# Strassen's algorithm for gate and up of a SwiGLU, and a down projection that adds in DRAM

## The chip, the core and the metric

The kernel runs on one core of one Trainium2 chip. The metric is device time in microseconds of one execution, the median of several runs. A core has five engines with instruction streams of their own: TensorE (PE in the profile; PEld is its weight load), VectorE (DVE), ScalarE (ACT), GpSimd (POOL) and SyncE (SP, which here only issues DMAs). Each takes its instructions in order, and semaphores tie them together.

## The reference

One decoder layer over 512 tokens in float32, width 2048. Two token mixers (windowed attention and gated linear attention) are merged and projected, and then comes the part that the change touches, a SwiGLU with 5632 hidden features:

```python
h = h + merged @ w_out[l]
z = rmsnorm(h, norm_ffn_g[l])
ff = (jax.nn.silu(z @ w_ffn_gate[l]) * (z @ w_ffn_up[l])) @ w_ffn_down[l]
h = h + ff
return rmsnorm(h, norm_final_g)
```

## The kernel before

Features lie on the 128 partitions and the 512 tokens on the free axis, so an activation is 16 tiles of 128x512. TensorE works on operands of about 12 significant bits (fp32r). Each float32 operand is therefore split into a high part (`wh`, `zh`, `fh`: a ScalarE cast) and a low part (`wl`, `zl`, `fl`: a VectorE subtraction), and each product takes three matmuls: hi x hi, hi x lo, lo x hi (`mm3`).

All weights come from DRAM as pieces of 128x1024 (512 KB), in the order of their use, on SP's queue. `load_piece` issues the DMA into `wf` and splits it into `wh` and `wl`; `next_piece` hands out a piece and asks for the second one behind it. There are three buffers of each kind. `project` makes two feature tiles out of four pieces: 24 matmuls of 512 tokens per piece.

The SwiGLU takes the hidden features in `NB` = 11 blocks of 512. `ffn_up` makes gate and up of a block in two halves of two feature tiles each (gate's two tiles, then up's two), with sigmoid and products behind them, and splits the result into `fh`, `fl`. `ffn_down` multiplies a block by the 512x2048 rows of the down weight, 16 output tiles of 12 matmuls, and VectorE adds each tile to `acc`, which stays in SBUF and is loaded from `h_d` (the residual, in DRAM) in block 0. The loop makes `ffn_up(blk + 1)` ahead of `ffn_down(blk)`, so that TensorE has work while a block's elementwise part ends. The last block goes by halves of 256 tokens. Its weights (`wfd`, `whd`, `wld`) are loaded and split while `ffn_down` of block 9 runs, and each half ends in the final norm.

The residual, the gained second-norm input `z` and its split are made behind the output projection `wo`, tile by tile (`hT`, `zh`, `zl`, and `hsq`, the sum of squares). The norm's inverse rms (`second_norm`) is applied behind the products. SBUF for activations is a pool of 66 long slots ("slot") and 12 short ones ("work") of 128x512. PSUM has four banks for products (`psm`) and four others. A scheduler orders the instructions of each engine, so the order in a queue isn't quite that of the code.

Of the kernel before, what the change touches and what calls it, by code (L numbers as in the profile page):

```python
# [19 lines left out]
P = 128  # L20
# [28 lines left out]
N_LONG, N_SHORT = 66, 12  # L49
# [4 lines left out]
def shape_constants():  # L54
    """Arrays that the shapes alone fix: which bias bucket a distance falls in, and masks."""
# [25 lines left out]
def weight_pieces(w_in, w_proj_a, w_proj_b, w_out, w_ffn_gate, w_ffn_up, w_ffn_down):  # L81
    """The weights in the order of their use, in pieces of [128, 1024]: partition p of a piece holds
    rows p, p + 128, ... of some rows and columns of a weight."""
# [30 lines left out]
    def up(blk):  # L114
        for c0 in (blk * T, blk * T + 2 * P):
            pair(w_ffn_gate, c0)
            pair(w_ffn_up, c0)

    up(0)
    for blk in range(NB):  # L120
        if blk + 1 < NB:
            up(blk + 1)
        for c0 in range(0, D, 2 * P):
            cut(w_ffn_down, blk * T, c0, 4, 2 * P)
    return np.stack(pieces)
# [3 lines left out]
def hybrid_layer(  # L129
# [24 lines left out]
    wpool = ctx.enter_context(tc.tile_pool(name="wpool", bufs=3))  # L154
# [6 lines left out]
    def slot(name, dtype=F32):  # L161
        return tpool.tile([P, T], dtype, tag="t", name=name)
# [23 lines left out]
    # the first use of ScalarE loads its table: ahead of the data  # L186
# [7 lines left out]
    def split(dst_hi, dst_lo, src):  # L194
        """src = hi + lo exactly, each of 12 significant bits."""
        nc.scalar.copy(dst_hi, src)  # L196
        nc.vector.tensor_tensor(out=dst_lo, in0=src, in1=dst_hi.bitcast(F32), op=ALU.subtract)  # L197

    n_last = D // (2 * P)
    n_pieces = pieces.shape[0] - n_last  # L200
    ahead = []

    def load_piece(i):
        wf = wpool.tile([P, CW], F32, tag="wf", name=f"wf_{i}")
        wh = wpool.tile([P, CW], F32R, tag="wh", name=f"wh_{i}")
        wl = wpool.tile([P, CW], F32R, tag="wl", name=f"wl_{i}")
        ahead.append((wh, wl))
        if i < KD // 2:
            return wf
        nc.sync.dma_start(wf, pieces[i])  # L210
        split(wh, wl, wf)

    taken = [0]
# [15 lines left out]
    def mm3(ps, ah, al, bh, bl, first, last):  # L229
        """ps += (ah + al).T @ (bh + bl)."""  # L230
# [4 lines left out]
    def project(rh, rl, name):  # L235
        """Two banks of (w[:, 256 columns].T @ r), features on partitions."""
# [11 lines left out]
    def inv_rms(ssq, n, name, cols=4):  # L248
        """(ssq / n + eps) ** -0.5 on a [128, cols] tile."""
# [8 lines left out]
    def across(r, name, cols=4):  # L258
        """[128 tokens, cols] -> a bank with the tokens' values on every partition."""
        bank = aux_bank(f"ps_b_{name}")  # L260
        for tt in range(cols):
            diag = small.tile([P, P], F32, tag="diag", name=f"diag_{name}_{tt}")
# [6 lines left out]
    def token_sums(sqs, name, cols=4):  # L269
        """Column sums of the sum of [128, 128 * cols] tiles, as [128 tokens, cols] in a bank."""  # L270
# [287 lines left out]
    def log_gates():  # L558
        """log(sigmoid(z)) = min(z, 0) - log(1 + exp(-|z|)), head by head."""
# [20 lines left out]
    def gla_values(c):  # L580
        """Values of heads 2c and 2c+1, tokens on partitions."""
# [15 lines left out]
    def scaled(banks, name):  # L597
        """What a projection left in banks, times each token's inverse rms."""
# [13 lines left out]
    def gla_gate(h, q, k, st):  # L612
        """Decayed queries and keys of a head, from its log gates summed in chunks."""
# [13 lines left out]
        # of each chunk in a pair: what its queries see a state through, what its keys reach one  # L627
        # through; and the pair's whole decay
# [30 lines left out]
    def gla_scores(h, st):  # L659
        """Scores inside a pair of chunks, keys on partitions; the state's keys, tokens there."""  # L660
# [25 lines left out]
    def gla_states(h, vs, st):  # L686
        """The state ahead of each pair of chunks."""
# [23 lines left out]
    def gla_outputs(h, vs, st):  # L711
        """Outputs, features on partitions, and their inverse rms."""
# [75 lines left out]
    def gated(yh, yl, m0, name):  # L788
        """sigmoid(gate) * (y @ w) for two feature tiles."""
# [29 lines left out]
    zh, zl = [], []  # L819
    hsq = slot("hsq")  # L820
    for m0 in range(0, KD, 2):
        for i, bank in enumerate(project(mh, ml, f"wo{m0}")):
# [5 lines left out]
            zh.append(slot(f"zh_{m}", F32R))  # L828
            zl.append(slot(f"zl_{m}", F32R))
            gcol = g_ffn_sb[:, m : m + 1]  # L830
            nc.scalar.activation(zh[m], hT, AF.Copy, scale=gcol)
            nc.vector.scalar_tensor_tensor(
                out=zl[m],
                in0=hT,
                scalar=gcol,
                in1=zh[m].bitcast(F32),
                op0=ALU.mult,
                op1=ALU.subtract,
            )
            if m == 0:  # L840
                nc.scalar.activation(hsq, hT, AF.Square)
            else:
                s2 = work(f"hsq_{m}")
                nc.scalar.activation(s2, hT, AF.Square)
                nc.vector.tensor_tensor(out=hsq, in0=hsq, in1=s2, op=ALU.add)

    def second_norm():
        rb = slot("rb2")
        nc.vector.tensor_copy(rb, across(inv_rms(token_sums([hsq], "ffn"), D, "ffn"), "ffn"))
        return rb  # L850

# [1 line left out]
    acc = [None] * KD  # L853
    rb2 = None

    def ffn_up(blk):
        fh, fl = [], []
        for pair in range(2):
            gs = []
            banks = project(zh, zl, f"fg{blk}_{pair}")  # L860
            if blk == 0 and pair == 0:
                nonlocal rb2
                rb2 = second_norm()
            for m, bank in enumerate(banks):
                g = work(f"g_{blk}_{pair}_{m}")
                nc.vector.tensor_tensor(out=g, in0=bank, in1=rb2, op=ALU.mult)
                s = work(f"gs_{blk}_{pair}_{m}")
                nc.scalar.activation(s, g, AF.Sigmoid)
                nc.vector.tensor_tensor(out=g, in0=g, in1=s, op=ALU.mult)
                gs.append(g)  # L870
            for m, bank in enumerate(project(zh, zl, f"fu{blk}_{pair}")):
                u = work(f"u_{blk}_{pair}_{m}")
                nc.vector.tensor_tensor(out=u, in0=bank, in1=rb2, op=ALU.mult)
# [142 lines left out]
```

## Time and profile before

| | |
|---|---|
| median of 3 runs | 2664.93 us (2664.81 to 2666.26) |
| the profiled execution | a span of 2663.9 us, the time of its engines' work; 2664.93 is 1.0 above it |
| TensorE | 99% of the span busy, clock 0.996 |
| VectorE, ScalarE, GpSimd | 45%, 28%, 1% |
| DMA | 280.73 MB, mean 105 GB/s |
| wf loads | 448 of 512 KB, median 3.7 us to landing |
| one SwiGLU block | 576 matmuls of 512 tokens, 0.2266 us from start to start (5296 in 1200 us): 130.5 us, a third of it the down projection |

The page gives totals first, then the span in 40 slices, the DMA queues, the chain of work that ended last, and the costliest groups. A row of a group ends in the count, the busy time, the mean duration in ns, and the idle time of the engine just ahead of it with what ended that. In a timeline row the start and the duration (us) come first. A row of a table by stretches gives each engine's busy time with its number of instructions in brackets, then the TensorE clock, the DMA share of 16 engines and GB/s. In a row on an operation's durations, three numbers are least, median and largest ns.

### The profile page before, as it was taken

The numbers are of one execution on the slowest core, as the hardware profiler recorded it, in microseconds if no ns is written. First come the engines' busy times: TensorE is split into PE (matmuls) and PEld (weight loads), VectorE is DVE, ScalarE is ACT, GpSimd is POOL, SyncE is SP. The second block draws the span as 40 slices with busy tenths as digits, with TensorE's granted clock in tenths as the row PEclk, the third lists the DMA queues.
The fourth block names the chain that finished last, engine by engine and source line by source line (L and its number), as shares of the span: only waits on it lengthen the run. The fifth ranks groups of instructions, "written<-read, shape, count | busy, mean of one in ns | idle before, by whom it ended". The sixth has DMA issues, their size and how long they took to land.

```text
span 2663.9 us, 29245 instructions
## 1 busy us (share of the span) xinstructions
PE 2635.0 (99%) x12038; PEld 2188.5 (82%) x12038; DVE 1185.7 (45%) x1690; ACT 753.0 (28%) x1040; POOL 21.4 (1%) x42
## 2 busy tenths in 40 slices
PE   8899999999999999999999999999999999999998
PEld 7777888888888888888888888888888888888887
DVE  6695463733333335444343434444434343434355
ACT  5465222422222223332222222222222222222233
POOL 0000000000000000000000000000000000000001
PEclk9999999999999999999999999999999999999999
DMA  6622223234433333443343233323323232233231
GB/s 193 130 71 71 80 87 95 72 127 133 127 111 111 108 98 107 142 147 103 99 141 117 95 98 101 95 95 96 102 95 95 96 101 96 95 96 102 95 124 67
DMA packets 92070, 280.73 MB, mean 105 GB/s; under 512 B 10512, under 2 KB 18880, under 8 KB 91936
## 3 DMA queue, kind: packets, MB, share of 16 engines
q1 hardware_dynamic: 91936, 278.87, 33.3%
q8 instruction: 94, 1.54, 0.2%
q14 instruction: 40, 0.33, 0.0%
HBM read 263.11 MB, written 15.72 MB: 105 GB/s over the span
## 4 chain that ended last, share of the span: by engine, by line
PE 96%; DMA 1%; DVE 1%; ACT 1%; issue 0%; POOL 0%; SPq 0%; DVEq 0%; ACTq 0%; POOLq 0%
PE ps_fd L232 6%; PE ps_fd L233 6%; PE ps_fd L231 6%; PE ps_fg L233 6%; PE ps_fg L231 6%; PE ps_fg L232 6%; PE ps_fu L233 6%; PE ps_fu L232 6%; PE ps_fu L231 6%; PE ps_ga L231 2%; PE ps_wo L233 2%; PE ps_gb L231 2%; PE ps_ga L232 2%; PE ps_wo L232 2%; PE ps_ga L233 2%; PE ps_gb L233 2%
## 5 line engine op out<-in xcount | busy, mean ns | idle before, releaser
L197 DVE TENSOR_TENSOR wl<-wf,wh 128x1024 fp32r<-128x1024 f32 (+1 forms) x464 | 559.0, 1205 | 1011.0 <-ACT wh L196 1002.6
L196 ACT CAST wh<-wf 128x1024 fp32r<-128x1024 f32 (+1 forms) x464 | 481.3, 1038 | 1535.6 <-PE ps_fd L232 315.5
L231 PE MATMUL ps_fu<-zh,wh 128*128 128x512 f32 x704 | 274.0, 389 | 0.0
L232 PE MATMUL ps_fu<-zl,wh 128*128 128x512 f32 x704 | 274.0, 389 | 0.0
L233 PE MATMUL ps_fu<-zh,wl 128*128 128x512 f32 x704 | 273.9, 389 | 0.0
L231 PE MATMUL ps_fg<-zh,wh 128*128 128x512 f32 x704 | 273.9, 389 | 0.0
L232 PE MATMUL ps_fg<-zl,wh 128*128 128x512 f32 x704 | 273.9, 389 | 0.0
L233 PE MATMUL ps_fg<-zh,wl 128*128 128x512 f32 x704 | 273.9, 389 | 0.0
L231 PE MATMUL ps_fd<-fh,wh 128*128 128x512 f32 x640 | 249.0, 389 | 0.0
L232 PE MATMUL ps_fd<-fl,wh 128*128 128x512 f32 x640 | 249.0, 389 | 0.0
L233 PE MATMUL ps_fd<-fh,wl 128*128 128x512 f32 x640 | 249.0, 389 | 0.0
L892 DVE TENSOR_TENSOR acc<-ps_fd,acc 128x512 f32<-128x512 f32 x160 | 110.5, 691 | 193.7 <-PE ps_fd L233 193.7
L232 PEld LDWEIGHTS ps_fg<-zl,wh 128*128 128x128 f32 x704 | 132.2, 188 | 27.4
L233 PEld LDWEIGHTS ps_fu<-zh,wl 128*128 128x128 f32 x704 | 132.2, 188 | 27.4
L233 PEld LDWEIGHTS ps_fg<-zh,wl 128*128 128x128 f32 x704 | 132.2, 188 | 27.4
L232 PEld LDWEIGHTS ps_fu<-zl,wh 128*128 128x128 f32 x704 | 132.2, 188 | 27.4
L231 PEld LDWEIGHTS ps_fg<-zh,wh 128*128 128x128 f32 x704 | 132.2, 188 | 27.4
L231 PEld LDWEIGHTS ps_fu<-zh,wh 128*128 128x128 f32 x704 | 132.2, 188 | 27.4
L231 PEld LDWEIGHTS ps_fd<-fh,wh 128*128 128x128 f32 x640 | 120.2, 188 | 25.0
L233 PEld LDWEIGHTS ps_fd<-fh,wl 128*128 128x128 f32 x640 | 120.2, 188 | 24.9
L232 PEld LDWEIGHTS ps_fd<-fl,wh 128*128 128x128 f32 x640 | 120.2, 188 | 24.9
L231 PE MATMUL ps_ga<-uh,wh 128*128 128x512 f32 x256 | 100.1, 391 | 0.0
(264 smaller groups left out, 3992.8 us busy)
## 6 DMA issues: line engine op xcount, KB each, us to landing
wf<-in_pieces_dram SPq DMA_DIRECT2D x448, 512.0 KB, 3.7
x<-in_xT_dram SPq DMA_DIRECT2D x16, 256.0 KB, 4.8
wf<-in_pieces_dram SPq DMA_DIRECT2D x16, 256.0 KB, 4.6
mA_d<-sga SPq DMA_DIRECT2D x16, 256.0 KB, 3.2
ya<-mA_d SPq DMA_DIRECT2D x16, 256.0 KB, 3.0
hT<-in_xT_dram SPq DMA_DIRECT2D x16, 256.0 KB, 3.6
h_d<-hT SPq DMA_DIRECT2D x16, 256.0 KB, 3.3
acc<-h_d SPq DMA_DIRECT2D x16, 256.0 KB, 4.8
```

The lines of the kernel that those rows point to most:

```text
L196: nc.scalar.copy(dst_hi, src)
L197: nc.vector.tensor_tensor(out=dst_lo, in0=src, in1=dst_hi.bitcast(F32), op=ALU.subtract)
L231: nc.tensor.matmul(ps, lhsT=ah, rhs=bh, start=first, stop=False)
L232: nc.tensor.matmul(ps, lhsT=ah, rhs=bl, start=False, stop=False)
L233: nc.tensor.matmul(ps, lhsT=al, rhs=bh, start=False, stop=last)
L892: nc.vector.tensor_tensor(out=acc[m], in0=bank, in1=acc[m], op=ALU.add)
```

## The change

Gate and up are computed by Strassen's algorithm for 2x2 blocks, in Winograd's form with seven products. The two halves of the tokens are the columns of one operand. The other operand is made of two feature tiles (even and odd) of the input by the two weights, gate and up. Each product has 256 tokens. A piece now holds a "quad": four 128-row tiles of gate and of up for one hidden tile.

- Weights. `load_quads` splits three of the four raw blocks (768 columns), makes four sums of 256 columns in place on VectorE, and splits all 1024 columns again into `th` and `tl`. `wh` and `wl` have four buffers, of which a quad takes two each; `wf` has two.
- Tokens. `strassen_side` makes from each pair of feature tiles of `z` four sums and seven split sides (`zs`) of 256 tokens. Three pairs (`KEPT` = 6 tiles) go into the output projection, five behind it. The norm of the mixers (`rb1`) is applied to `z`, and `second_norm` divides it out again.
- Products. `ffn_pair(blk, j)` makes one hidden tile of gate and up out of four quads: 7 x 2 x 3 = 42 matmuls of 256 tokens per quad, 168 per pair. It needs all four banks of `psm`. A ScalarE copy and seven VectorE operations of 256 combine them into `g` and `up`, and then come the five operations of 512 (scalings, products, split).
- Down. ScalarE copies each bank to a work slot, and GpSimd issues a DMA that adds it to `h_d` in DRAM. `acc` is loaded from there once, behind the last block.
- Order. The loop makes pair 0 of the next block, then down of this block, then pairs 1 to 3 of the next. Ahead of the last halves stand three pairs where a down projection stood.

```diff
-N_LONG, N_SHORT = 66, 12
+N_LONG, N_SHORT = 66, 11
+KEPT = 6
...
-    wpool = ctx.enter_context(tc.tile_pool(name="wpool", bufs=3))
+    wpool = ctx.enter_context(tc.tile_pool(name="wpool", bufs=4))
...
+    def load_quads(i, wf, wh, wl):
+        nc.sync.dma_start(wf, pieces[i])
+        split(wh[:, 0 : 6 * P], wl[:, 0 : 6 * P], wf[:, 0 : 6 * P])
+        b11, b21, b22, b12 = (wf[:, n * 2 * P : (n + 1) * 2 * P] for n in range(4))
+        tt = nc.vector.tensor_tensor
+        tt(out=b11, in0=b11, in1=b12, op=ALU.add)
+        tt(out=b12, in0=b12, in1=b22, op=ALU.add)
+        tt(out=b22, in0=b11, in1=b22, op=ALU.add)
+        tt(out=b21, in0=b22, in1=b21, op=ALU.add)
+        th = wpool.tile([P, CW], F32R, tag="wh", name=f"th_{i}")
+        tl = wpool.tile([P, CW], F32R, tag="wl", name=f"tl_{i}")
+        split(th, tl, wf)
...
+    def strassen_side(j, za, zb):
+        s12, s34 = work(f"s12_{j}"), work(f"s34_{j}")
+        tt = nc.vector.tensor_tensor
+        tt(out=s12[:, one], in0=zb[:, two], in1=za[:, two], op=ALU.subtract)
+        tt(out=s12[:, two], in0=s12[:, one], in1=za[:, one], op=ALU.add)
+        tt(out=s34[:, one], in0=za[:, one], in1=za[:, two], op=ALU.subtract)
+        tt(out=s34[:, two], in0=s12[:, two], in1=zb[:, one], op=ALU.subtract)
...
+        for i, side_ in enumerate(sides):
+            t = slot(f"zs_{j}_{i}", F32R)
+            split(t[:, one], t[:, two], side_)
...
+        if m0 < KEPT:
+            strassen_side(m0 // 2, *pair)
+        else:
+            late.append((m0 // 2, *pair))
+    for pair in late:
+        strassen_side(*pair)
...
+    def ffn_pair(blk, j):
+        b4 = [mm_bank(f"ps_fu{blk}_{j}_{i}") for i in range(4)]
...
+        for k0 in range(0, KD // 2, 2):
+            raw, sums = next_quads()
+            for i, (hl, at) in enumerate(
+                ((raw, 0), (raw, 1), (raw, 2), (sums, 0), (sums, 3), (sums, 2), (sums, 1))
+            ):
...
+                for kp in range(2):
+                    z = zs[k0 + kp][i]
+                    wh, wl = (t[:, at, kp] for t in hl)
...
+                    nc.tensor.matmul(bank, lhsT=wh, rhs=z[:, one], start=first, stop=False, skip_group_check=True)
+                    nc.tensor.matmul(bank, lhsT=wh, rhs=z[:, two], start=False, stop=False, skip_group_check=True)
+                    nc.tensor.matmul(bank, lhsT=wl, rhs=z[:, one], start=False, stop=last, skip_group_check=True)
...
+        nc.scalar.copy(u[:, one], outs[0])
+        tt(out=g[:, one], in0=outs[1], in1=u[:, one], op=ALU.add)
+        tt(out=u[:, one], in0=u[:, one], in1=outs[5], op=ALU.subtract)
+        tt(out=u[:, two], in0=outs[4], in1=u[:, one], op=ALU.add)
+        tt(out=g[:, two], in0=outs[6], in1=u[:, two], op=ALU.add)
+        tt(out=up[:, two], in0=outs[3], in1=u[:, two], op=ALU.add)
+        tt(out=u[:, one], in0=outs[3], in1=u[:, one], op=ALU.add)
+        tt(out=up[:, one], in0=outs[2], in1=u[:, one], op=ALU.add)
+        tt(out=g, in0=g, in1=rb2, op=ALU.mult)
+        s = work(f"gs_{blk}_{j}")
+        nc.scalar.activation(s, g, AF.Sigmoid)
...
-                if blk == 0:
-                    acc[m] = slot(f"acc_{m}")
-                    nc.sync.dma_start(acc[m], h_d[m])
-                nc.vector.tensor_tensor(out=acc[m], in0=bank, in1=acc[m], op=ALU.add)
+                part = work(f"fd_{blk}_{m}")
+                nc.scalar.copy(part, bank)
+                nc.gpsimd.dma_start(h_d[m], part, accum_op=ALU.add)
-    ff = ffn_up(0)
+    ff = [ffn_pair(0, j) for j in range(4)]
     for blk in range(NB - 1):
-        nxt = ffn_up(blk + 1)
-        ffn_down(blk, *ff)
+        nxt = [ffn_pair(blk + 1, 0)]
+        ffn_down(blk, ff)
+        nxt += [ffn_pair(blk + 1, j) for j in range(1, 4)]
         ff = nxt
+    acc = []
+    for m in range(KD):
+        acc.append(slot(f"acc_{m}"))
+        nc.sync.dma_start(acc[m], h_d[m])
```

The instructions of each engine move as follows at three places.

First, VectorE's queue before, in gate and up of block 5 (`wl_n` is the low part of piece n). Each piece is one row, and the elementwise work of a tile (L866, L869) stands between pieces.

```order
L197 TENSOR_TENSOR wl_314_12495<-wf_314_12493,wh_314_12494 128x1024
L197 TENSOR_TENSOR wl_315_12525<-wf_315_12523,wh_315_12524 128x1024
L197 TENSOR_TENSOR wl_316_12555<-wf_316_12553,wh_316_12554 128x1024
L197 TENSOR_TENSOR wl_317_12585<-wf_317_12583,wh_317_12584 128x1024
L866 TENSOR_TENSOR g_5_0_0_12613<-ps_fg5_0_0_12491,rb2_8789 128x512
L869 TENSOR_TENSOR g_5_0_0_12613<-g_5_0_0_12613,gs_5_0_0_12615 128x512
```

The same queue after, where quads 307 and 308 are prepared and pair 1 of block 4 has ended.

```order
L209 TENSOR_TENSOR tl_306_14606<-wf_306_14595,th_306_14605 128x1024
L209 TENSOR_TENSOR wl_307_14653<-wf_307_14651,wh_307_14652 128x768
L238 TENSOR_TENSOR wf_307_14651<-wf_307_14651 128x256
L239 TENSOR_TENSOR wf_307_14651<-wf_307_14651 128x256
L240 TENSOR_TENSOR wf_307_14651<-wf_307_14651 128x256
L241 TENSOR_TENSOR wf_307_14651<-wf_307_14651 128x256
L209 TENSOR_TENSOR tl_307_14662<-wf_307_14651,th_307_14661 128x1024
L209 TENSOR_TENSOR wl_308_14709<-wf_308_14707,wh_308_14708 128x768
L957 TENSOR_TENSOR g_4_2_14820<-ps_fu4_2_0_14591,uu_4_2_14819 128x256
L238 TENSOR_TENSOR wf_308_14707<-wf_308_14707 128x256
```

A quad takes six rows, of which `tl` waits for ScalarE's `th`, which is made of what L241 wrote; the combinations of a pair (L957 and on) stand between the rows of the next pair's first quads.

Second, VectorE's queue where the output projection ends, before.

```order
L826 TENSOR_TENSOR hT_14_8645<-ps_wo14_0_8523,hT_14_8645 128x512
L832 SCALAR_TENSOR_TENSOR zl_14_8650<-hT_14_8645,g_ffn_sb_7513,zh_14_8649 128x512
L845 TENSOR_TENSOR hsq_7516<-hsq_7516,hsq_14_8653 128x512
L197 TENSOR_TENSOR wl_202_8671<-wf_202_8669,wh_202_8670 128x1024
L826 TENSOR_TENSOR hT_15_8656<-ps_wo14_1_8524,hT_15_8656 128x512
```

And after: the last token side ends there, and behind it stands the first VectorE row of the third quad. Between z_15 and these rows stand the other rows of the five late sides.

```order
L209 TENSOR_TENSOR zs_7_3_8855<-s12_7_8840,zs_7_3_8855 128x256
L209 TENSOR_TENSOR zs_7_4_8858<-s34_7_8841,zs_7_4_8858 128x256
L209 TENSOR_TENSOR zs_7_5_8861<-s12_7_8840,zs_7_5_8861 128x256
L209 TENSOR_TENSOR zs_7_6_8864<-z_15_8727,zs_7_6_8864 128x256
L209 TENSOR_TENSOR wl_202_8873<-wf_202_8871,wh_202_8872 128x768
```

Piece 202, whose split stood ahead of the last residual tile, now stands behind 55 rows of token sides.

Third, SP's queue at the end, before and after (wf_455 is the last piece of the loop, wfd_n the last block's weights).

```order
L210 DMA wf_455_17237<-in_pieces_dram 128x1024
L906 DMA wfd_0_17329<-in_pieces_dram 128x1024
L906 DMA wfd_1_17339<-in_pieces_dram 128x1024
L906 DMA wfd_2_17349<-in_pieces_dram 128x1024
L906 DMA wfd_3_17359<-in_pieces_dram 128x1024
```

```order
L234 DMA wf_455_22700<-in_pieces_dram 128x1024
L1007 DMA wfd_0_22895<-in_pieces_dram 128x1024
L1007 DMA wfd_1_22905<-in_pieces_dram 128x1024
L999 DMA acc_0_22861<-h_d_7515 128x512
L999 DMA acc_1_22863<-h_d_7515 128x512
```

wf_455 was a piece of a down projection and is now the last quad of the last pair. Sixteen acc loads stand between wfd_1 and wfd_2.

More of the change, by code (lines that the diff above doesn't have):

```diff
@@ L845, in hybrid_layer @@
                 nc.vector.tensor_tensor(out=hsq, in0=hsq, in1=s2, op=ALU.add)
-    def second_norm():
[L848 to L853, printed above, removed]
-    rb2 = None
[L856 to L873, printed above, removed]
-                nc.vector.tensor_tensor(out=u, in0=u, in1=gs[m], op=ALU.mult)
-                fh.append(slot(f"fh_{blk}_{pair}_{m}", F32R))
-                fl.append(slot(f"fl_{blk}_{pair}_{m}", F32R))
-                split(fh[-1], fl[-1], u)
```

101 lines of the change are left out of this document (77 added, 24 removed).

## The prediction

> **What bounds the kernel now.** I read the page's totals and chain first, then a table by stretches, then single instructions for prices.
>
> ```profile
> span 2663.9 us, 29245 instructions
> PE 2635.0 (99%) x12038; PEld 2188.5 (82%) x12038; DVE 1185.7 (45%) x1690; ACT 753.0 (28%) x1040; POOL 21.4 (1%) x42
> PE 96%; DMA 1%; DVE 1%; ACT 1%; issue 0%; POOL 0%; SPq 0%; DVEq 0%; ACTq 0%; POOLq 0%
> core 0: us, PE busy (x) PEld busy (x) DVE busy (x) ACT busy (x) POOL busy (x), PEclk, DMA share, GB/s
> 1300.00:2500.00 1200.00, 1200.00 (x5296) 993.98 (x5295) 490.52 (x549) 277.35 (x295) 0.00 (x0) 1.00 0.31 100
> 2025.07 1.22 DVE L197 TENSOR_TENSOR wl<-wf,wh 128x1024 fp32r<-128x1024 f32 x1 [4.21 <-ACT wh L196]
> 2030.47 1.23 DVE L197 TENSOR_TENSOR wl<-wf,wh 128x1024 fp32r<-128x1024 f32 x1 [4.17 <-ACT wh L196]
> ```
>
> TensorE is the chain: 96% of it, and in 1200 us of SwiGLU it is never idle, at the full clock. A 512-token matmul there costs 1200/5296 = 0.2266 us from start to start. The last two rows are consecutive weight pieces in gate/up: VectorE works 1.2 us per piece and waits 4.2. So removed matmul time counts in full until something else fills a piece's 5.4 us. The profiled span is 2663.9 against a median of 2664.9 for the runs, so I sum on the span and add 1.0.
>
> **What TensorE saves.** Matmul and weight-load durations overlap, so the pitch must be read from starts.
>
> ```profile
> 2600.61 0.28 PE L231 MATMUL ps_fd<-fh,whd 128*128 128x256 f32 x1
> ...
> 2603.00 0.28 PE L233 MATMUL ps_fd<-fh,wld 128*128 128x256 f32 x1
> L232 PEld LDWEIGHTS ps_fd<-fl,whd 128*128 128x128 f32 x128 | 24.6, 192 | 0.0
> ```
>
> These are the first and the 21st of the 256-token matmuls in the last block: 2.39/20 = 0.1195 us. Gate and up now take 11 blocks x 4 feature tiles x 2 weights x 48 = 4224 matmuls, 957.1 us. The change makes 11 x 4 x 168 = 7392 of 256 tokens, 883.3 us: 73.8 us less TensorE work. A quad (42 matmuls) is 5.02 us, a feature tile of gate and up (four quads, a "pair" below) 20.1 instead of 21.75.
>
> **What VectorE gains.** Prices:
>
> ```profile
> L197 DVE TENSOR_TENSOR wl<-wf,wh 128x1024 fp32r<-128x1024 f32 x448 | 548.2, 1224 | 1009.6 <-ACT wh L196 1001.2 <-PE ps_att L663 8.4
> L197 DVE TENSOR_TENSOR wld<-wfd,whd 128x512 fp32r<-128x512 f32 x16 | 10.4, 686 | 3.0 <-ACT whd L196 3.0
> L946 DVE TENSOR_TENSOR acc<-ps_fd,acc 128x256 f32<-128x256 f32 x32 | 13.5, 423 | 3.4 <-PE ps_fd L233 1.0
> L196 ACT CAST wh<-wf 128x1024 fp32r<-128x1024 f32 x448 | 471.7, 1053 | 1531.6 <-PE ps_fd L232 315.5 <-PE ps_fg L232 299.3 <-PE ps_fu L232 203.2
> L196 ACT CAST whd<-wfd 128x512 fp32r<-128x512 f32 x16 | 9.1, 617 | 7.2 <-DMA wfd<-in_pieces_dram 7.2
> 1991.53 0.69 DVE L873 TENSOR_TENSOR u<-ps_fu,rb 128x512 f32<-128x512 f32 x1
> 1992.26 0.69 DVE L874 TENSOR_TENSOR u<-u,g 128x512 f32<-128x512 f32 x1
> 1992.87 1.22 DVE L197 TENSOR_TENSOR wl<-wf,wh 128x1024 fp32r<-128x1024 f32 x1
> 1994.00 0.68 DVE L197 TENSOR_TENSOR fl<-u,fh 128x512 fp32r<-128x512 f32 x1
> 2023.99 1.05 ACT L196 CAST wh<-wf 128x1024 fp32r<-128x1024 f32 x1 [4.39 <-PE ps_fu L232]
> ```
>
> The 768-column forms lie midway between 512 and 1024: 0.955 us for the subtraction, 0.835 for the cast (estimates). Starts show how operations follow each other: a dependent one starts 0.04 us after its producer's end (1991.53 to 1992.26), an independent one 0.08 before its predecessor's (1992.87 to 1994.00 = 1.13), and ScalarE to VectorE costs 0.03 (2023.99 + 1.05 to 2025.07).
>
> A quad asks of VectorE: the low part wl (0.955), four additions (0.423 each), and the low part tl (1.224), 3.87 us busy. But in the order of the queue VectorE also waits inside each quad, since tl needs ScalarE's cast th, which needs the last addition, and the next quad's wl stands behind tl. The cycle is 1.13 (tl) + 0.995 (wl) + 3 x 0.463 + 0.423 + 0.03 (additions) + 1.053 + 0.03 (th) = 5.05 us, against TensorE's 5.02: no slack at all. At each pair's end come seven combinations of 256 (0.423) and five operations of 512 (about 0.69), 6.4 us, which in queue order partly fill two of the waits. Stepping through those rows with the three spacings gives 13.5 us for the two quads around a boundary instead of 10.1: +3.4, say 3.5. So a pair is 4 x 5.05 + 3.5 = 23.7 us: slower than the 20.1 of TensorE, and than the 21.75 of before.
>
> The down projection keeps its 43.5 us (192 matmuls of 512) and gives the chain a rest, during which two quads are made ready; four slots of split weights hold no more. From its end: 18 matmuls free the first slot (2.2), a cast (0.87), 14 quads (70.7), three boundaries (10.5), and 24 matmuls on the last quad's sums (2.9) = 87.2 us for the four pairs up to the next down projection, against 4 x 21.75 = 87.0. So **+0.2 per block, +2 for the nine** full ones; the last three pairs by the same count 63.5 against 65.3, **-2**.
>
> **The start.** Five of the eight token sides stand on VectorE behind the last output projection, ahead of wl_202, the third quad. That is hT, z and hsq (2.1 us) and 55 operations of 256, at 0.34 (independent) to 0.46 (dependent), 0.38 on average, 20.9: wl_202 starts some 24 us after the last matmul (23.0 and the waits for ScalarE's casts). Two quads (10.1) and the second norm's small operations (1.2) later tl_203 is done, then 2.9 of matmuls: the first pair ends at 38 instead of 21.75, **+16.5**. The next four pairs run in the chain without a rest, 4 x (23.7 - 21.75) = **+8**.
>
> **The end.** Before, the last block's weights are made under the down projection of block 9, which now stands three pairs earlier.
>
> ```profile
> L197 DVE TENSOR_TENSOR wld<-wfd,whd x16: 681/685/694, 2581.1 to 2601.1; 128x512 fp32r<-128x512 f32 x16
> L906 SPq DMA_DIRECT2D wfd<-in_pieces_dram x8: 327/328/328, 2575.7 to 2594.9; - x8
> L891 SPq DMA_DIRECT2D acc<-h_d x16: 378/383/430, 1379.3 to 1401.6; - x16
> 10.00:20.00 10.00, 10.00 (x46) 8.27 (x45) 9.88 (x17) 10.00 (x19) 0.00 (x0) 1.00 1.05 390
> ```
>
> Now nothing lies between the last pair and its down projection: the copy out of PSUM, combinations, sigmoid, products and split, about 7 us one after the other, are idle time of TensorE. Beside them SP issues wfd_1, sixteen acc loads (0.38 each, 6.1 us) and then wfd_2 onward, two at a time: 7.9 MB, 20 us at the 390 GB/s of the last row, so the weights come in just ahead of a half's 192 x 0.1195 = 23 us of matmuls. I take **+8**: 7 and one late tile.
>
> **Loads, accumulating DMAs, and what I cost at nothing.**
>
> ```profile
> DMA to landing us min/median/max: 3.4/3.7/4.9
> wf<-in_pieces_dram SPq DMA_DIRECT2D x448, 512.0 KB, 3.7
> h_d<-hT SPq DMA_DIRECT2D x16, 256.0 KB, 3.3
> acc<-h_d SPq DMA_DIRECT2D x16, 256.0 KB, 4.8
> L892 DVE TENSOR_TENSOR acc<-ps_fd,acc 128x512 f32<-128x512 f32 x160 | 110.5, 691 | 193.7 <-PE ps_fd L233 193.7
> L735 ACT COPY ob<-ps_ob 128x512 f32<-128x512 f32 x8 | 4.7, 586 | 4.0 <-PE ps_ob L727 4.0
> 1378.00:1403.00 25.00, 25.00 (x112) 20.72 (x111) 14.44 (x18) 5.46 (x6) 0.00 (x0) 1.00 0.71 245
> DMA to landing us min/median/max: 3.8/3.9/4.5
> ```
>
> The first row is wf from 1300 to 2500. With two wf buffers, one buffer's round is landing + 6.1 (casts, subtractions, additions, hops) for two quads; it stays inside 10.1 while landing is under 4.0, so 3.7 just fits. The last two rows, of 1378 to 1403, are the 25 us in which sixteen acc loads ran beside the weights: share 0.71, landing 3.9. The 160 accumulating DMAs come one per 2.7 us, under the down projection. No row shows such a DMA; at the least it costs a write (3.3), at the most a read and a write in turn (8.1). With eleven work slots I take them as hidden, 0, nearest the write, since the 16 of a block have 130 us until the next. The Trainium skill, "DMA: Bandwidth & Descriptors", section "Anatomy of one DMA — SWDGE (gpsimd) path", gives a DMA from GpSimd 2.0 us plus its bytes at 436 GB/s: 2.6 us here, an estimate, by which the sum would stay the same. No run here shows one.
>
> Removed from VectorE are the 160 additions L892 (0.69); they were covered by TensorE, so nothing. ScalarE gets 160 copies of 0.59 in their place, in a stretch where it is a quarter busy. GpSimd's queue holds nothing else there. Three token sides in the output projection (some 4.4 us each) go into VectorE's idle half. If the cover, 43.5 us of matmuls, fell away, these copies would cost about 9 us a block.
>
> **Sum.** 16.5 + 8 + 2 - 2 + 8 = +32.5: span 2696, time **2697 us**. The 73.8 us of TensorE are turned into waiting for the split weights.
>
> **Rivals.** (A) TensorE sets the pace, because VectorE's rows overlap better than I stepped them: -73.8 + 16.5 + 8 = -49, 2616. It decides once a quad's cycle is under about 4.83 us (then 14 x 0.22 = 3.1 us less per block, 11 blocks, cancels the 32). For it: the margin is 0.2 us in 5, and my 768-wide prices are interpolated; so is that 15.5 + 6.4 = 21.9 us of VectorE per pair shrink to 19.0 if each of its 36 operations overlapped the one before by 0.08; against it: the additions depend on each other and tl on ScalarE, and then none of that overlap is to be had. (B) Weights land late under the accumulating traffic: at 4.5 us a quad costs (4.5 + 6.1)/2 = 5.3, +0.25 for some 164 quads, +41, 2738; at 5.0, 2779. For it: a maximum of 4.9; against: 3.9 beside the acc loads. (C) Accumulating DMAs go one after the other at 8.1 us or more and keep the work slots that L957 and the sigmoid need: 130 us a block is the edge; at 9, 14 us a block, about 2840. (D) A cycle of 4.8 to 5.0: 2655 to 2685.
>
> (E) The weight load bounds a 256-token matmul: 192 ns each, 7392 x 0.192 = 1419, +462, 3127; the 0.1195 between starts speaks against it, since those rows load a new weight for each matmul too. The Trainium skill, "TensorE: Matmul & The Clock Gate", section "Back-to-back issue gap", says that the spacing in a stream of loads and matmuls is set by both operations. The trace agrees only as far as the 0.1195 already holds both.
>
> **Chances.** The forecast (2685 to 2715) 0.52; A 0.15; D 0.12; B 0.14; C 0.06; E 0.01. The range, 2640 to 2775, leaves out most of A, C and E and the end of B. A measurement of this kernel tells 0.2%, 5 us, from no change: faster takes A and a third of D, 0.19; same, the lower middle of D, 0.08; slower the rest, 0.73.
>
> **What the profile after would show.** If I am right: TensorE's idle time grows to about 7 us per block between the down projections, ended by VectorE's wl and tl; tl starts about 5.05 us apart inside a pair and VectorE over 85% busy between the down projections; 16 us of idle after the last output projection, ended by tl; about 7 us ahead of the last block's halves; down projections without gaps, and accumulating DMAs landing in 3 to 8 us. If A holds, TensorE is gapless between the down projections. If B, ScalarE's wh waits for the DMA; if C, L957 or the sigmoid waits for an accumulating DMA. My forecast is wrong above all if pairs take other than 23 to 24.5 us in the chain.

## The result, and the profile after

The changed kernel takes 2698.36 us (median of 4 runs, 2697.92 to 2701.17) against 2665.09 of before in the same runs: a ratio of 1.0127, 95% interval 1.0113 to 1.0142. That is 33 us slower; the forecast was 2697. The profiled execution, the slowest of the four by 2.5 us or more, has a span of 2699.4 us, 35.5 over that of before.

The page's totals, then the down projection of block 3 and the four pairs behind it, and the first matmul of each end of that stretch:

```profile
span 2699.4 us, 37980 instructions
PE 2610.9 (97%) x15206; PEld 2300.6 (85%) x15206; DVE 1635.9 (61%) x2808; ACT 986.9 (37%) x1460; POOL 160.2 (6%) x202
1729.90:1773.45 43.55, 43.55 (x195) 36.05 (x193) 19.73 (x28) 19.00 (x27) 12.99 (x15) 1.00 0.88 193
1773.45:1860.50 87.05, 83.74 (x673) 81.40 (x672) 71.05 (x125) 32.48 (x41) 0.86 (x1) 1.00 0.35 96
1773.45 0.28 PE L948 MATMUL ps_fu<-zs,wh 128*128 128x256 f32 x1
1860.53 0.40 PE L270 MATMUL ps_fd<-fh,wh 128*128 128x512 f32 x1
```

The totals mislead here: TensorE still reads 97% busy, because a 256-token matmul is recorded with 0.28 us of which 0.12 count. The stretch shows the state of things: VectorE is busy for 71 of 87 us, and the stretch, 672 matmuls that need 80.3 us, takes 87.1. One quad of it on VectorE:

```profile
1786.26 1.23 DVE L209 TENSOR_TENSOR tl<-wf,th 128x1024 fp32r<-128x1024 f32 x1 [1.19 <-ACT th L208]
1787.40 0.95 DVE L209 TENSOR_TENSOR wl<-wf,wh 128x768 fp32r<-128x768 f32 x1
1788.39 0.42 DVE L238 TENSOR_TENSOR wf<-wf 128x256 f32<-128x256 f32 x1
...
1789.77 0.43 DVE L241 TENSOR_TENSOR wf<-wf 128x256 f32<-128x256 f32 x1
1791.39 1.23 DVE L209 TENSOR_TENSOR tl<-wf,th 128x1024 fp32r<-128x1024 f32 x1 [1.19 <-ACT th L208]
```

From tl to tl 5.13 us pass (5.05 forecast), with the wait of 1.19 us for ScalarE's th ahead of each tl. The groups say how much that wait is in all, and how little the weights' landing is:

```profile
L209 DVE TENSOR_TENSOR tl<-wf,th 128x1024 fp32r<-128x1024 f32 x176 | 215.5, 1224 | 185.2 <-ACT th L208 181.7 <-PE ps_fu L950 2.4 <-PE ps_fu L949 1.2
L208 ACT CAST wh<-wf 128x768 fp32r<-128x768 f32 x176 | 146.5, 833 | 69.3 <-PE ps_fd L271 34.1 <-DMA wf<-in_pieces_dram 17.3 <-ACT fd L987 7.3
h_d<-fd POOLq DMA_DIRECT2D x160, 256.0 KB, 5.9
```

The start and the end, as a table by stretches and as matmuls with the idle time ahead of them:

```profile
1216.50:1229.40 12.90, 0.97 (x11) 0.89 (x9) 12.90 (x39) 7.29 (x23) 0.00 (x0) 0.59 0.00 1
1229.40:1236.00 6.60, 5.83 (x33) 5.41 (x34) 4.54 (x12) 1.78 (x2) 1.11 (x1) 0.77 0.13 12
1229.39 0.58 PE L950 MATMUL ps_fu<-zs,wl 128*128 128x256 f32 x1 [11.93 <-DVE wl L209]
2627.49 0.58 PE L270 MATMUL ps_fd<-fh,whd 128*128 128x256 f32 x1 [5.61 <-ACT whd L208]
2627.50:2634.00 6.50, 6.50 (x37) 6.48 (x38) 3.40 (x7) 1.92 (x4) 0.00 (x0) 0.66 1.05 395
```

At 1216.5 TensorE has used up the two quads that were ready, and for 12.9 us VectorE is full of token sides while TensorE stands; at 2621.9 it stands for 5.6 us while the last pair is combined. (The row names whd because the first cast of the last block's weights stands right behind that of fh in ScalarE's queue and ends last.) After both the granted clock is down (0.77, 0.66).

From the starts of the first matmuls of each stage, in the two profiled executions:

| stage | before | after | difference |
|---|---|---|---|
| first five pairs, to the first down matmul (before: 177.0 for eight, less 65.3 for three) | 111.7 | 132.2 | +20.5 |
| nine stretches of four pairs, mean | 87.04 | 87.25 (86.5 to 88.6) | +0.2 each, +1.9 |
| ten down projections | 43.52 | 43.55 | +0.3 |
| last three pairs | 65.3 | 63.3 | -2.0 |
| from there to the end | 63.3 | 77.5 | +14.2 |

With 0.6 us ahead of the SwiGLU this is the 35.5 of the spans.

### The profile page after: what moved, and what is told of

Read it like the earlier page. It is cut to its first block, busy times and chain, and to the rows that moved or that the text cites. A ratio compares the mean times of both kernels' runs of the same rounds, so it can differ in the third digit from the quotient of the medians.

```text
span 2699.4 us, 37980 instructions
## 1 busy us (share of the span) xinstructions
PE 2610.9 (97%) x15206; PEld 2300.6 (85%) x15206; DVE 1635.9 (61%) x2808; ACT 986.9 (37%) x1460; POOL 160.2 (6%) x202
## 5 line engine op out<-in xcount | busy, mean ns | idle before, releaser
L209 DVE TENSOR_TENSOR wl<-wf,wh 128x1024 fp32r<-128x1024 f32 (+2 forms) x464 | 511.4, 1102 | 656.0 <-ACT wh L208 652.1
L208 ACT CAST wh<-wf 128x1024 fp32r<-128x1024 f32 (+2 forms) x464 | 442.3, 954 | 823.1 <-DMA wf<-in_pieces_dram 172.9
L948 PE MATMUL ps_fu<-zs,th 128*128 128x256 f32 x1408 | 400.5, 287 | 16.2 <-ACT th L208 14.0
L950 PE MATMUL ps_fu<-zs,tl 128*128 128x256 f32 x1408 | 393.4, 288 | 14.1 <-DVE tl L209 14.0
L949 PE MATMUL ps_fu<-zs,th 128*128 128x256 f32 x1408 | 395.4, 283 | 0.0
L209 DVE TENSOR_TENSOR tl<-wf,th 128x1024 fp32r<-128x1024 f32 x176 | 215.5, 1224 | 185.2 <-ACT th L208 181.7
L948 PE MATMUL ps_fu<-zs,wh 128*128 128x256 f32 x1056 | 301.4, 288 | 6.5 <-ACT wh L208 5.4
L950 PE MATMUL ps_fu<-zs,wl 128*128 128x256 f32 x1056 | 292.8, 285 | 15.2 <-DVE wl L209 15.2
L949 PE MATMUL ps_fu<-zs,wh 128*128 128x256 f32 x1056 | 296.7, 283 | 0.0
L948 PEld LDWEIGHTS ps_fu<-zs,th 128*128 128x128 f32 x1408 | 269.7, 192 | 24.0 <-ACT th L208 21.0
L950 PEld LDWEIGHTS ps_fu<-zs,tl 128*128 128x128 f32 x1408 | 264.8, 192 | 23.2 <-DVE tl L209 23.2
L949 PEld LDWEIGHTS ps_fu<-zs,th 128*128 128x128 f32 x1408 | 270.0, 192 | 0.0
L948 PEld LDWEIGHTS ps_fu<-zs,wh 128*128 128x128 f32 x1056 | 202.9, 192 | 15.1 <-ACT wh L208 11.8
L950 PEld LDWEIGHTS ps_fu<-zs,wl 128*128 128x128 f32 x1056 | 199.8, 193 | 17.5 <-DVE wl L209 17.5
L949 PEld LDWEIGHTS ps_fu<-zs,wh 128*128 128x128 f32 x1056 | 203.1, 192 | 0.4
```

The source lines that it names most:

```text
L948: nc.tensor.matmul(bank, lhsT=wh, rhs=z[:, one], start=first, stop=False, skip_group_check=True)
L949: nc.tensor.matmul(bank, lhsT=wh, rhs=z[:, two], start=False, stop=False, skip_group_check=True)
L950: nc.tensor.matmul(bank, lhsT=wl, rhs=z[:, one], start=False, stop=last, skip_group_check=True)
```

## The experiments

The theory to test is that of the prediction, called the split chain: VectorE in queue order, with its wait for th, sets the pace of gate and up. Its rivals are the loads (landing of the weights, beside the adding DMAs) and the matmuls themselves. The stretch lengths below are from the first gate and up matmul behind a down projection to the first matmul of the next, mean of nine.

**The additions left out.**

```diff
-        tt(out=b11, in0=b11, in1=b12, op=ALU.add)
-        tt(out=b12, in0=b12, in1=b22, op=ALU.add)
-        tt(out=b22, in0=b11, in1=b22, op=ALU.add)
-        tt(out=b21, in0=b22, in1=b21, op=ALU.add)
```

> The four additions of each quad are left out, so th and tl split the raw blocks and the result is not the layer's. Split chain (VectorE with its wait for ScalarE sets the pace of gate and up): a quad's cycle falls from 5.1 us by the additions (1.84) and the wait for th, to under the 5.02 of TensorE; the stretch between two down projections goes from 87.2 to 80.3 to 82 us, the start and the last three pairs gain some 20 together, and the time is about 2625 us, faster than before the change. Matmuls (256-token matmuls and their semaphores set the pace): stretches stay at 87, the time at 2695 to 2700. Loads (landing of weights sets it): the buffer's round shortens too, so a gain speaks for the chain or the loads together, and the third kernel of this set separates them no further; the plain write does.

2615.61 us, 0.9816 of before (0.9800 to 0.9833), some 10 us better than expected, and stretches of 80.62 us. One of them:

```profile
1735.80:1816.20 80.40, 80.40 (x673) 80.40 (x672) 51.10 (x69) 35.39 (x43) 0.86 (x1) 1.00 0.39 113
```

VectorE has 20 us less to do, and TensorE runs 673 matmuls in 80.4 us without a gap: 0.1195 each. The matmuls are not the limit, and 80.6 is the floor of any version with these 672 matmuls. The first five pairs went from 132.2 to 115.2.

**Plain writes in place of adding DMAs.**

```diff
-                nc.gpsimd.dma_start(h_d[m], part, accum_op=ALU.add)
+                nc.gpsimd.dma_start(h_d[m], part)
```

> GpSimd's DMAs write the parts of the down projection over h_d in place of adding them, so the sums and the residual are lost; number, size and order of the DMAs stay. Split chain: the DMAs are hidden, the time stays within 5 us of 2698. Loads: the adding DMAs (median 5.9 us to landing, share of the 16 engines 0.88 in a down projection) delay the weights; a plain write lands in some 3.3 to 4 us, the waits of wh for wf behind a down projection shorten, and the time falls by 10 to 20 us.

2697.1 us (2696.03 to 2698.44), stretches 87.19: no change that can be told.

```profile
h_d<-fd POOLq DMA_DIRECT2D x160, 256.0 KB, 2.5
```

A plain write of 256 KB lands in 2.5 us and an adding one in 5.9, and yet nothing waits for the difference. Adding in DRAM is hidden, as taken. The loads rival loses its first cause.

**Sums in two halves.** The blocks lie in the order in which their sums are ready, so that ScalarE casts the first 512 columns of th during the last two additions.

```diff
-            block = np.stack([t1[:, 0], t1[:, 1], t2[:, 1], t2[:, 0]])
+            block = np.stack([t2[:, 0], t1[:, 0], t2[:, 1], t1[:, 1]])
...
-        split(wh[:, 0 : 6 * P], wl[:, 0 : 6 * P], wf[:, 0 : 6 * P])
-        b11, b21, b22, b12 = (wf[:, n * 2 * P : (n + 1) * 2 * P] for n in range(4))
+        split(wh[:, 2 * P :], wl[:, 2 * P :], wf[:, 2 * P :])
+        b12, b11, b22, b21 = (wf[:, n * 2 * P : (n + 1) * 2 * P] for n in range(4))
...
-        split(th, tl, wf)
+        for c in (slice(0, T), slice(T, CW)):
+            split(th[:, c], tl[:, c], wf[:, c])
...
-                ((raw, 0), (raw, 1), (raw, 2), (sums, 0), (sums, 3), (sums, 2), (sums, 1))
+                ((raw, 1), (raw, 3), (raw, 2), (sums, 1), (sums, 0), (sums, 2), (sums, 3))
```

> The same computation; the blocks of a quad lie in the order in which their sums are ready (b12, b11, b22, b21), and th and tl are made in two halves of 512 columns, so that ScalarE casts the first half during the last two additions. Split chain: the wait for th (1.19 us in each quad's row) goes, a cycle is 0.995 + 1.81 + about 1.3 = 4.1 us; VectorE's work of a pair is 4 x 4.1 + 5.4 = 21.8, the stretch between down projections 80.5 to 82.5, the start gains 8 to 10, the last pairs 2 to 3; the time is 2630 to 2645, faster than before the change. Loads or matmuls: the time stays at 2690 or above.

2642.52 us, 0.9917 of before (0.9902 to 0.9932), stretches 82.65: 56 us less, with no less work. Between the two profiled executions the difference is 58.7: 41.4 in the nine stretches, 9.8 in the first five pairs, 1.4 in the last three, and 5.6 at the end, which this edit doesn't touch.

```profile
L209 DVE TENSOR_TENSOR tl<-wf,th 128x512 fp32r<-128x512 f32 x352 | 240.3, 685 | 61.1 <-ACT th L208 54.7
L208 ACT CAST wh<-wf 128x768 fp32r<-128x768 f32 x176 | 146.7, 833 | 122.4 <-DMA wf<-in_pieces_dram 51.1 <-PE ps_fd L272 36.7 <-PE ps_fu L950 19.0
1749.50:1832.20 82.70, 81.20 (x672) 80.59 (x672) 71.17 (x139) 36.50 (x57) 0.86 (x1) 1.00 0.36 104
```

The wait of tl for th falls from 181.7 to 54.7 us. VectorE's busy time in a stretch is the 71 us of before this edit, and even a little more instructions; only the order in which it can start them has changed. The second row names the next limit: wh now waits 51.1 us for weights to land, where it had been 17.3.

**The late token sides left out.**

```diff
-    for pair in late:
-        strassen_side(*pair)
+    for j, za, zb in late:
+        zs[j] = zs[j % 3]
```

> The five late token sides are left out; their products take the sides of the first three pairs of features instead, so the result is not the layer's. Everything else stays. If the sides on VectorE's queue behind the output projection are what the start costs (predicted 16.5 us of the first pair, 20 measured for the first five pairs together), the first pair ends some 14 to 17 us earlier and the time is 2680 to 2685 us; the later stretches stay at 87. If the second norm or the first quads' weights set the start, it stays at 2695 or more.

2681.12 us (2676.72 to 2683.03), 17 us less; the first five pairs take 114.5 in place of 132.2, the stretches 87.22 as before.

```profile
1205.40:1230.00 24.60, 24.13 (x199) 23.71 (x197) 18.61 (x35) 8.56 (x11) 1.11 (x1) 1.00 0.37 107
```

TensorE no longer stands (12.9 us in the changed kernel), and its clock stays at 1.00. Those 55 rows are 17.6 of the 20.5 us that the start lost.

**The tail: the order of the acc loads, then more buffers.** Two acc loads behind each weight load in place of sixteen behind the second:

```diff
         nc.sync.dma_start(wf, pieces[n_pieces + i])
+        for m in (2 * i, 2 * i + 1):
+            acc.append(slot(f"acc_{m}"))
+            nc.sync.dma_start(acc[m], h_d[m])
```

> The sixteen acc loads are asked for two at a time behind each of the last block's weights, in place of all between the second and the third. The tail cost 14 us more than before (8 predicted): 5.7 us of idle ahead of the halves and 28.5 us for a half of 23.2. If the acc loads ahead of the weights made the half late, it takes 23 to 25 us, and the time falls by 3 to 6 us. If the two buffers of the weights did, it stays.

2695.66 us (2694.31 to 2697.46), a gain of 2.7, little more than the runs scatter, and none of it in the first half: 28.0 us from its first to its last matmul, against 28.2. The order wasn't the cause. Then the weights in six buffers that the last quads leave:

```diff
-        wf = wpool.tile([P, CW], F32, tag="wf", name=f"wfd_{i}", bufs=2)
+        tag = ("wf", "wf", "wh", "wl", "wh", "wl", "wh", "wl")[i]
+        wf = wpool.tile([P, CW], F32, tag=tag, name=f"wfd_{i}", bufs=2 if tag == "wf" else 4)
```

> Six of the last block's eight weight loads go into the buffers of wh and wl, which the last quads leave, in place of two buffers of wf in turn; the acc loads then stand behind them all in SP's queue. The order of the acc loads alone moved the half not at all (28.4 us against 28.5), so if the two buffers made it late, the first half now takes 23 to 24 us of matmuls and the time falls by 5 to 7 us to about 2692; the 5.6 us of idle ahead of the halves stay, since they are the elementwise chain of the last pair.

2692.75 us (2690.82 to 2695.83), as expected, but the half at 25.5, where 23 to 24 were.

```profile
2628.20:2654.00 25.80, 25.75 (x192) 25.59 (x192) 20.86 (x46) 16.44 (x35) 0.00 (x0) 0.89 0.49 182
```

TensorE is now busy throughout the half, but its clock is 0.89 over it, and 0.11 of 25.8 is about the 2.6 us left over 22.9: the half begins at a low clock after 5.6 us of idle. The two buffers are not the whole cause of the other 2.7, though. In the run with the sums in halves, with the same two buffers and the same order of loads, the half took 25.6 us, and ScalarE waited 1.76 us for the third weight load in place of 4.07. What made that load land earlier there wasn't tested.

**Two products on GpSimd.**

```diff
-        tt(out=g, in0=g, in1=s, op=ALU.mult)
-        tt(out=up, in0=up, in1=rb2, op=ALU.mult)
+        nc.gpsimd.tensor_tensor(out=up, in0=up, in1=rb2, op=ALU.mult)
+        nc.gpsimd.tensor_tensor(out=g, in0=g, in1=s, op=ALU.mult)
```

> The same computation; two of the five 512-wide products at each pair's end (up by the norm, gate by its sigmoid) go from VectorE to GpSimd. Split chain: a pair's boundary on VectorE falls from 3.4 us by two operations of 0.6 to 0.68, the stretch between down projections from 87.2 to 83 to 84 us, the start and the end together 5; the time is 2655 to 2665. Rival, from the Trainium skill, SBUF — State Buffer, section Who interferes with whom, a VectorE operation with two SBUF inputs and a GpSimd operation that reads SBUF exclude each other: VectorE's additions and subtractions beside the products wait, by up to the 1.4 us of each product (twice the 0.75 that GpSimd took for 256 columns), the 44 x 2 products cost up to what they saved or more, and the time is 2695 to 2750. The durations of VectorE's rows beside GpSimd's tell which.

2741.49 us (2739.56 to 2742.66), 43 us slower than the changed kernel; stretches 90.96.

```profile
1813.39 1.22 DVE L209 TENSOR_TENSOR tl<-wf,th 128x1024 fp32r<-128x1024 f32 x1
1814.53 0.42 DVE L963 TENSOR_TENSOR u<-ps_fu,uu 128x256 f32<-128x256 f32 x1
1814.87 1.94 DVE L209 TENSOR_TENSOR wl<-wf,wh 128x768 fp32r<-128x768 f32 x1
1818.00 0.69 DVE L970 SCALAR_TENSOR_TENSOR u<-u,g 128x512 f32<-128x512 f32 x1 [1.19 <-POOL u L968]
1814.71 1.29 POOL L969 TENSOR_TENSOR g<-g,gs 128x512 f32<-128x512 f32 x1 [23.09 <-ACT gs L967]
1815.96 2.00 POOL L968 TENSOR_TENSOR u<-u,rb 128x512 f32<-128x512 f32 x1
```

wl takes 1.94 us beside the first product, where it takes 0.95 alone, and ends at 1816.8, about when it would have ended (1817.0) had it begun behind that product. Then L970 waits 1.19 for the second. The rival by the Trainium skill ("SBUF — State Buffer", section "Who interferes with whom") is what happened: two SBUF inputs on VectorE and a reading GpSimd operation exclude each other. The groups of the whole run agree:

```profile
L209 DVE TENSOR_TENSOR wl<-wf,wh 128x768 fp32r<-128x768 f32 x176 | 188.7, 1072 | 83.2 <-ACT wh L208 83.1
L965 DVE TENSOR_TENSOR g<-g,rb 128x512 f32<-128x512 f32 x44 | 43.1, 980 | 0.0
L963 DVE TENSOR_TENSOR u<-ps_fu,uu 128x256 f32<-128x256 f32 x44 | 18.3, 417 | 0.0
L970 DVE SCALAR_TENSOR_TENSOR u<-u,g 128x512 f32<-128x512 f32 x44 | 30.4, 690 | 48.9 <-POOL g L969 26.4 <-POOL u L968 22.5
```

In the changed kernel wl took 167.8 us and L965 30.1, both with two SBUF inputs; L963, with one input in PSUM, took the same 18.4. The two products had cost VectorE 60.3 us, and L970 alone now waits 48.9 for them. The chain alone, which counted the two operations as gone, was wrong here.

**The down projection's change alone**, on the kernel before.

```diff
-                nc.vector.tensor_tensor(out=acc[m], in0=bank, in1=acc[m], op=ALU.add)
+                part = work(f"fd_{blk}_{m}")
+                nc.scalar.copy(part, bank)
+                nc.gpsimd.dma_start(h_d[m], part, accum_op=ALU.add)
...
+    for m in range(KD):
+        acc[m] = slot(f"acc_{m}")
+        nc.sync.dma_start(acc[m], h_d[m])
```

> The kernel before with the second part of the change alone: ScalarE copies each down tile out of PSUM, GpSimd adds it to DRAM, and acc is loaded once, behind the last block's weights. Predicted cost nothing: 0 to +3 us on 2665, all of it at the end, where the last acc loads wait for the last adding DMAs (5.9 us to landing). If the adding DMAs or the copies disturb the stream of weights, +10 or more, spread over the ten down projections.

2667.57 us (median of 11 runs, 2664.29 to 2670.49), 1.0007 of before (0.9998 to 1.0016): no difference that can be told. In the profiled execution (2669.49) the stretches are the 87.04 of before, and the first half takes 27.6 in place of 22.9, though not for the acc loads:

```profile
2606.33 0.39 PE L231 MATMUL ps_fd<-fh,whd 128*128 128x256 f32 x1 [2.96 <-ACT fd L890]
2604.66 1.14 ACT L196 CAST whd<-wfd 128x512 fp32r<-128x512 f32 x2 [1.27 <-DMA wfd<-in_pieces_dram]
2605.70 1.07 ACT L890 COPY fd<-ps_fd 128x512 f32<-128x512 f32 x2
```

TensorE stands 2.96 us until block 9's last down tiles are copied out of PSUM. Those copies stand in ScalarE's queue behind casts of the last block's weights, which wait for their loads (a median of 6.7 us to landing, 4.2 before); the clock is 0.64 over the 4.7 us behind. Whether the adding DMAs made the loads late isn't shown.

**A third buffer for wf**, first with the halves and the tail's buffers, then alone. It costs two of the eleven short slots.

```diff
-N_LONG, N_SHORT = 66, 11
+N_LONG, N_SHORT = 66, 9
...
-        wf = wpool.tile([P, CW], F32, tag="wf", name=f"wf_{i}", bufs=2)
+        wf = wpool.tile([P, CW], F32, tag="wf", name=f"wf_{i}", bufs=3)
```

> The same computation: th and tl in two halves, the last block's weights in the buffers of wh and wl, and three buffers of wf (short slots 9 in place of 11). With two, wh of a quad waited 51 us in all for wf to land once the sums were split in halves. Loads: with a third buffer these waits go and the stretch between down projections falls from 82.5 to 81 to 81.5 us, the time to 2622 to 2632. Split chain: the waits lie beside VectorE's own work; the stretch stays at 82.5, the time at 2638 to 2642. If nine short slots are too few for the parts that the adding DMAs read, the combinations at a pair's end wait for them and the time rises.

2611.65 us, 0.9799 of before (0.9783 to 0.9815), the fastest of all, and 10 us better than the best end of what was expected. The stretches stand at 80.71, all nine within 0.1.

```profile
1732.33:1812.88 80.55, 80.55 (x673) 80.53 (x672) 72.18 (x140) 36.86 (x58) 0.86 (x1) 1.00 0.39 116
```

TensorE has no gap, and the stretch is at the floor of the first experiment, with all of VectorE's 72 us in it. Against the halves alone (30.9 us): nine stretches 17.5, the first five pairs 4.5, the last three 1.1, and 7.3 that I had not expected ahead of the SwiGLU, where the output projection ends at 1198.0 in place of 1205.3. Alone:

> The changed kernel with three buffers of wf (short slots 9 in place of 11) and nothing else. Together with the sums in halves the third buffer brought 26 to 31 us, of which 7 before the SwiGLU and 1.8 in each of nine stretches. Split chain: without the halves VectorE's cycle of 5.1 us stays, so the stretch between down projections stays at 86.5 to 87.2, and only the 7 us before the SwiGLU and one or two at each end are gained: 2684 to 2692. Loads: the weights' landing was the limit in the changed kernel too, the stretch falls to 84 or less, the time to 2660 or less.

2687.4 us (2684.88 to 2688.53), stretches 86.70 (86.6 to 86.9). So in the changed kernel the loads made the difference between 86.7 and the 87.25 of its stretches, and the scatter of those, and no more; the 5 us per stretch belong to VectorE's wait for th. Only when that wait is taken away are two buffers the limit. Most of the other 6 us gained lie ahead of the SwiGLU, which begins at 1198.7 in place of 1205.7.

**The start, twice more.** With halves and the tail's buffers, the sums of two late sides were made early:

```diff
+            sums = side_sums(m0 // 2, *pair) if m0 // 2 in EARLY else ()
-            late.append((m0 // 2, *pair))
+            late.append((m0 // 2, *pair, *sums))
```

> The same computation: th and tl in two halves, the last block's weights in the buffers of wh and wl, and the four sums of two of the five late token sides made during the output projection. From the single edits: 2642.5 less 1 to 3 at the end (the first half still stood at 25.8 there) and less 8 x 0.38 = 3 at the start, 2636 to 2640. If the start is set by something else than VectorE's work, only the end gains.

2637.51 us (2636.5 to 2638.59), 5 less than the halves; 2.2 of it at the start (122.34 to 120.15). And on the best version the last two sides were put behind the third quad:

```diff
-    for pair in late:
+    for pair in late[:3]:
         strassen_side(*pair)
...
             raw, sums = next_quads()
+            if blk == 0 and j == 0 and k0 == 0:
+                for pair in late[3:]:
+                    strassen_side(*pair)
```

> The same computation: sums in halves, three buffers of wf, the last block's weights in the buffers of wh and wl, and the last two of the five late token sides put behind the preparation of the third quad. VectorE's work at the start stays the same, but TensorE gets the third quad some 7 us earlier, so less is left when VectorE is done: 3 to 5 us less than 2611.7, 2606 to 2609. If VectorE's total alone sets when the first blocks end, since the chain behind takes what is gained, it stays at 2611.

2612.72 us (2611.58 to 2614.45): nothing gained on 2611.65. The first 37 us of the SwiGLU, there and in the version without this edit:

```profile
1197.60:1235.00 37.40, 30.38 (x204) 28.90 (x203) 34.79 (x92) 19.94 (x49) 1.11 (x1) 0.82 0.20 57
1198.00:1235.00 37.00, 26.85 (x200) 26.42 (x200) 34.72 (x91) 19.93 (x49) 1.11 (x1) 0.82 0.19 58
```

TensorE's busy time there is spread differently, but 204 and 200 matmuls were done, VectorE was busy for 34.8 of 37 us in both, and the first five pairs end 117.8 us after they began in both. Work that is put later on the full engine is still on it.

## Why the prediction came out

- **TensorE's saving** was right: the pitch of 0.1195, read from starts and not from durations, is the 80.4 us for 673 matmuls of the kernel without additions.
- **VectorE's cycle** was right, 5.13 us measured against 5.05, and so was the pair: from the second pair's first matmul to the first down projection 95.2 us for four, 23.8 each, against 23.7. The stretches came out at 87.25, forecast 87.2. That the wait in queue order, and not VectorE's busy time, is the cause is shown by the sums in halves: the same work, 4.6 us less per stretch.
- **The start** was forecast at +24.5 and measured at +20.5. The second pair begins after 37.0 us (38.2 forecast). The term that was off is the other side: I set 21.75 us a pair against it and overlooked what the second norm costs TensorE in the kernel before (177.0 us for eight pairs, 3.0 more than 8 x 21.75). In the changed kernel that norm is made beside the sides.
- **The end** was forecast at +8 and measured at +14.2 in the profiled run (+11.4 in the plain-write kernel, whose end has the same code). The idle time was 5.6, not 7. The mis-sized step is "the weights come in just ahead of a half": the half took 28.2 us from first to last matmul in place of 22.9. Some 2.7 us of that went when the loads had more than two buffers (25.5), though they went with the sums in halves too (25.6); the other 2.6 go with a low clock behind the idle gap (0.66 over 6.5 us), a cost that the sum doesn't have at all. The last 3.3 go with a wait between the halves and a second stretch at a low clock behind it (0.65 from 2657.8 to 2662.5), which the run of the plain writes doesn't have.
- **Nothing for the adding DMAs** was right (no change with plain writes, none clear of the scatter for the down part alone), though their 5.9 us lay between the two ends, and not at the nearer of them. **Nothing for the landing** was nearly right: 17.3 us of waits, and 0.5 us per stretch that a third buffer takes away. Two of the signs were off: VectorE was busy for 82% of the time between the down projections, not over 85, and the idle time after the output projection was 12 us ended by wl, not 16 ended by tl.

The two errors of 4 and 6 us have opposite signs; that the total (2698 against 2697) lies closer than its terms is luck. The rivals A (TensorE sets the pace) and E (the weight load does) are refuted by the same stretch: TensorE can do it in 80.4 and took 87.1. B didn't occur either: the weights landed in a median of 3.7 us as before, and plain writes changed nothing. With the sums in halves landing is the next limit, which one more buffer takes away. C didn't occur, since no row of L957 or the sigmoid waits for an adding DMA, and the 5.13 us lie outside D's 4.8 to 5.0.

## What to carry to other kernels

An algorithm with fewer multiplications pays in additions on another engine, so price the other engine in queue order, with its waits, and not by its busy share: 71 of 87 us busy was already the limit, and casting in two halves gained 53 us in gate and up without removing any work. Once the wait was gone, the next limit was one buffer away, and together with the tail's buffers they turned 1.27% slower into 2.0% faster than before. Before moving work to an idle engine, look for what it shares with the busy one; and behind each idle gap of TensorE add the time that the matmuls behind it take at a low clock.

## What the runs showed of the hardware

- The clock falls behind a gap of TensorE: after 11.9 us of idle the granted clock was 0.77 over the next 6.6 us, and after 5.6 us 0.66 over 6.5, with matmuls of 256 tokens starting 0.21 us apart. If these are means of half and full clock, the half clock lasted some 3.0 and 4.4 us after the gap. The Trainium skill, "TensorE: Matmul & The Clock Gate", section "What's actually happening", gives half the clock after an idle window of about 3.4 us, and the full one again after such a busy window; these two gaps agree with it roughly. But in the changed kernel the clock also fell behind two short waits, of 1.20 and 0.52 us, and stayed at 1.00 behind one of 1.19 at 2470.7, so an idle time of 3.4 us isn't needed:

```profile
2107.39 0.39 PE L948 MATMUL ps_fu<-zs,th 128*128 128x256 f32 x1 [1.20 <-ACT th L208]
2108.65 0.39 PE L950 MATMUL ps_fu<-zs,tl 128*128 128x256 f32 x1 [0.52 <-DVE tl L209]
2109.80:2113.00 3.20, 3.20 (x17) 3.20 (x17) 1.97 (x5) 0.98 (x2) 0.00 (x0) 0.50 0.37 145
```

- An adding DMA of 256 KB lands in 5.9 us and a plain one from the same queue in 2.5.
- A GpSimd product of 512 columns took 1.29 and 2.00 us beside a busy VectorE, and VectorE's operation with two SBUF inputs ended behind the first (0.95 us alone, 1.94 beside it); operations with one input in PSUM kept their 0.42.
- On VectorE, 256-column operations start 0.335 us apart when they are independent (L960 to L965 of the changed kernel, from 2622.19 to 2623.20) and 0.46 when each needs the one before or overwrites what that one reads (L238 to L241 above). Mixing two chains, as the scheduler did at the pairs' ends, makes the same operations a quarter cheaper.
